# Block 2's local attention split into scores, division and values, and an earlier read-back of its outputs

## The chip, the cores and the metric

One Trainium2 chip, one core. The metric is the device time in microseconds of one launch of the whole program: the median of the runs shown, and the time of the profiled execution beside it.

## The reference

Two transformer blocks over 1024 tokens of width 1024, in float32. Block 1 is a linear-recurrence branch, a differential attention and a mixture of experts; the change doesn't touch it. Block 2 projects the normed input to queries, keys and values of two attentions, joins their outputs, projects them back and ends in an MLP of width 4096. The attention that the change is about has 8 query heads on 2 key heads, blocks of 128 queries, and sees the block itself and the one before:

```python
def swa_sinks_attention(q, k, v, sinks):
    ...
    scores = jnp.einsum('bnqkgd,bnskd->bnkgqs', qb, kb).astype(jnp.float32) * scale
    ...
    scores = scores + alibi[None, None]
    scores = jnp.where(valid[None, :, None, None], scores, -jnp.inf)
    ...
    m = jnp.maximum(jnp.max(scores, axis=-1, keepdims=True), sink)
    p = jnp.exp(scores - m)
    denom = jnp.sum(p, axis=-1, keepdims=True) + jnp.exp(sink - m)
    p = (p / denom).astype(v.dtype)
    out = jnp.einsum('bnkgqs,bnskd->bnqkgd', p, vb)
...
def second_block(x, ...):
        ...
        out_a = swa_sinks_attention(qa, ka, va, sink_logits)
        ...
        out_b = forgetting_attention(qb, kb, vb, log_f)
        mixed = jnp.concatenate([out_a.reshape(b, s, A_Q_W), out_b.reshape(b, s, B_W)], axis=-1)
        x = x + jnp.einsum('bse,ed->bsd', mixed, w_out)
        hn = rmsnorm(x, mlp_norm_g)
        hid = jnp.square(jax.nn.relu(jnp.einsum('bsd,df->bsf', hn, w_up)))
        x = x + jnp.einsum('bsf,fd->bsd', hid, w_down)
```

## The kernel before, in words

**Order of the work.** No scheduler of the language decides the order. The kernel is written as Python generators ("tasks", class `Tasks`, L424). When the program is built, a planner (class `Model`, L40, and class `Engine`, L207) keeps an estimated clock for each engine, runs the task of the smallest priority number whose next operands it holds to be ready, and appends the instructions to the engines' streams. What a task yields is either a time (operands ready) or a condition. On the chip every engine then works through its own fixed stream and waits where an operand is late. The dense products of block 2 belong to the task of priority 9 and so fill what the attention tasks leave; the splitting of weights into two halves for the products (`Stream._split`, L589: one ACT copy, one DVE subtraction of 128x1024) is held back while ACT or DVE have much work queued by the planner's clock.

**Precision.** Each operand of a product is split into a high and a low part (a Copy on ACT, a subtraction on DVE: `split`, `split_T`), and each product is three matmuls, hh, hl, lh.

**Block 2** (`block2`, L2007) goes over the two halves of 512 tokens. In each half it makes the keys, values and queries of both attentions. `fox(half)` and `fox_values(half)` (L2296, L2415) are the full-length forgetting attention, `swa(half)` (L2165) the local one. All write their outputs to the DRAM tensor `d_mix`; `mixin(half)` (L2489) reads them back as eight 128x512 slices, splits each, and sets a flag, on which `out2(half)` (L2522) makes the output projection. Then the MLP of the first half (`mlp`, L2583) runs while `swa(1)` and then `fox(1)` are worked in between its products; `fox(1)` starts only after `swa(1)`.

**Inside `swa`** (L2165 to L2294), for a block n of 128 queries:

- `prep(n)` (L2208): 4 transposes of the queries, split into `t`.
- `scores(n)` (L2219): two steps z of 12 matmuls for 2 heads of both key heads; for each head a reduction on DVE (scale, bias, minimum; CUSTOM_DVE in the profile, 128x256), a small DVE multiplication, and an Exp on ACT that also sums the row.
- `values(n, kh)` (L2248), for each of two key heads: a sink term, a sum, a reciprocal and one DVE multiplication of 128x1024 that divides the probabilities; then for each of 2 key blocks 4 transposes and a split (ACT 128x512, DVE 128x512); then 4 matmuls, an ACT copy and a DVE addition of 64x512, and the store to `d_mix`.

One generator does all this in one sequence, since `nsr = 2` (L2172): the probabilities have two buffers, so `values(n-1, 0)`, `values(n-1, 1)` are finished before `scores(n)` begins:

```python
        for n in range(n0, n0 + 5):
            if n > n0 and nsr == 2:
                for kh in range(2):
                    yield from values(n - 1, kh)
            if n < n0 + 4:
                yield from scores(n)
```

`mixin(0)` is added as a task at L2087, after the values of half 1 have been projected, and waits for `swa0` or the first pair of heads of `fox(0)` (L2492).

Of the kernel before, what the change touches and what calls it, by code (L numbers as in the profile page):

```python
# [285 lines left out]
class Buf:  # L286
# [25 lines left out]
    def free(self):  # L312
        self.arena.release(self)
# [344 lines left out]
class Kern:  # L658
# [1348 lines left out]
    def block2(self):  # L2007
        F, R, io, v, act = self.F, self.R, self.io, self.v, self.act
# [58 lines left out]
        ready = lambda tt: lambda: self.has(f"x2T{tt}")  # L2067
        for half in range(2):
# [16 lines left out]
            if half == 0:  # L2085
                self.tasks.add(self.fox(0), 1)
            else:  # L2087
                self.tasks.add(self.mixin(0), 4)
                nq = 2
                yield from self.dense_N(U["qa", 1], lhs, banks, evac_norm(self.QA, True), tts=tts[:nq])  # L2090
                yield from self.out2(0)
                tts = tts[nq:]
# [3 lines left out]
            if half == 0:  # L2096
                self.tasks.add(self.swa(0), 2)
        for b in (ring, raws, sm, bf, self.r2):
            b.free()
# [65 lines left out]
    def swa(self, half):  # L2165
# [4 lines left out]
        n0 = 4 * half  # L2170
        k0 = max(n0 - 1, 0)
        nsr = 2  # L2172
        nk = n0 + 4 - k0
        yield lambda: (self.has(f"qa{half}") and self.ws.settled() and self.F.fits(256 * nk, 512, 512, 32, 32, 32, 32, 512, *[1024] * nsr) and
                       self.R.fits(256 * nk, 256 * nk, 1024, 1024, 1024, 1024))
        S, tb, ob = Banks(self.psum, 2, 2), Banks(self.psum, 4, 2), self.bank(6)
        kT, V = R.alloc(2 * 128 * nk), R.alloc(256 * nk)
# [3 lines left out]
        qr, qT, pt = Ring(F, 2, 512), Ring(R, 2, 1024), Ring(R, 2, 1024)  # L2181
        st, orr = Ring(F, 4, 32), Ring(F, 1, 512)
        self.sp.dma_start(kv.f(nk, 256), self.KVA[k0 * 128:(n0 + 4) * 128].rearrange("(a p) c -> p a c", p=128))
        qs, Q, P = {}, {}, {}

# [19 lines left out]
        kv.free()  # L2205
        sr = Ring(F, nsr, 1024)

# [11 lines left out]
        def scores(n):  # L2219
# [4 lines left out]
            ks = slice(e - w, e)  # L2224
            bs, ss = [sr.next(), sr.next()], [st.next(), st.next()]
            for z in range(2):
# [18 lines left out]
            for kh in range(2):  # L2245
                P[n, kh] = (bs[kh], ss[kh], w)

        def values(n, kh):  # L2248
            b, s, w = P.pop((n, kh))
            f = s.f()  # L2250
            x = b.f(4, 256)[:, :, :w]
            yield W(f)
            v.tensor_tensor(f[:, 8:12], f[:, 8:12], snk.f()[:, 4 * kh:4 * kh + 4], OP.add)
            act.activation(f[:, 8:12], f[:, 8:12], AF.Exp)
            v.tensor_tensor(f[:, 8:12], f[:, 8:12], f[:, 4:8], OP.add)
            v.reciprocal(f[:, 12:16], f[:, 8:12])
            v.tensor_tensor(x, x, f[:, 12:16, None].to_broadcast([128, 4, w]), OP.mult)
            yield W(b.f())
            nb = w // 128
            ts = []  # L2260
            for c in range(nb):
                p, t = tb.next(), pt.next()
                yield free(p)
                for j in range(4):
                    self.pe.transpose(p[:, j * 128:j * 128 + 128], b.f(4, 256)[:, j, c * 128:c * 128 + 128], self.ident)
                self.split_T(p, t.r(2, 512)[:, 0], t.r(2, 512)[:, 1], t.f(2, 512)[:, 0])
                ts.append(t)
            yield max(W(ts[-1].f()), free(ob))
            for c in range(nb):
                vv = V.r(nk, 2, 128)[:, n + 1 - nb + c - k0, kh]  # L2270
                self.mm(ob, vv, ts[c].r(2, 512)[:, 0], c == 0, False)
                self.mm(ob, vv, ts[c].r(2, 512)[:, 1], False, c == nb - 1)
            yield W(ob)
            t = orr.next()
            act.activation(t.f()[0:64], ob[64:128], AF.Copy)
            v.tensor_tensor(t.f()[0:64], t.f()[0:64], ob[0:64], OP.add)
            self.sp.dma_start(self.MIX[256 * kh:256 * kh + 256, n * 128:n * 128 + 128].rearrange("(h d) t -> d h t", d=64),
                              t.f(4, 128)[0:64])

        yield from prep(n0)  # L2280
        for n in range(n0, n0 + 5):
            if n > n0 and nsr == 2:
                for kh in range(2):
                    yield from values(n - 1, kh)
            if n < n0 + 4:
                yield from scores(n)
                if n + 1 < n0 + 4:
                    yield from prep(n + 1)
            if n > n0 and nsr == 4:
                for kh in range(2):  # L2290
                    yield from values(n - 1, kh)
        for b in (kT, V, qr, qT, sr, pt, st, orr) + ((bias, snk, g) if half else ()):
            b.free()
# [195 lines left out]
    def mixin(self, half):  # L2489

        F, R = self.F, self.R
        yield lambda: self.has(f"swa{half}") or self.has(f"fox{half}0")  # L2492
        yield lambda: F.fits(512, 512, 512) and R.fits(*([1024] * 6 if half else [8192]))
# [335 lines left out]
```

## Time and profile before

| | |
|---|---|
| median of 3 runs | 2784.4 us (2781.36 to 2788.27) |
| the profiled execution | 2780.47 us, its span 2778.7 us |
| PE busy | 2642.0 us, 95% of the span |
| DVE busy | 1785.0 us, 64% |
| ACT busy | 1507.8 us, 54% |
| mean granted TensorE clock | 0.979 |

PE is TensorE's matmuls, PEld its weight loads, DVE is VectorE, ACT is ScalarE, POOL is GpSimd, SP is SyncE, which issues the DMAs. Since almost all work on chip passes two helper lines (L234 for TensorE, L270 for the other engines), work is told apart by tiles and shapes and by where it stands in the streams. Block 2 begins near 1527 us. The bounds of its stages, used below, were found by counting TensorE's instructions from the end of the program: the streams of the built kernel and of the trace agree there instruction for instruction. A busy time is that of a profile: an instruction may start a little before the one ahead of it has ended.

### The profile page before, as it was taken

What the parts mean: (1) busy time and instruction counts of PE and PEld (TensorE: products, weight loads), DVE (VectorE), ACT (ScalarE), POOL (GpSimd) and SP (SyncE); (2) the same over time, 40 slices, a digit from 0 to 9 for tenths busy, and PEclk for the clock granted to TensorE, in tenths of its full rate; (3) what the DMA queues carried; (4) which work ended last, traced back from release to release, by engine and by line L of the source; (5) the groups of instructions that cost most, each with busy time, mean ns of one, the idle gap of its engine ahead of it and who ended that gap; (6) DMA issues with size and microseconds to landing.
All of it is one profiled execution on the core that took longest, in us unless ns stands there. A gap on an engine that the chain in (4) does not pass through costs nothing. (4 is left out here: it accounts for less than half of the span.)

```text
span 2778.7 us, 37066 instructions
## 1 busy us (share of the span) xinstructions
PE 2642.0 (95%) x13090; PEld 2146.4 (77%) x13090; DVE 1785.0 (64%) x3100; ACT 1507.8 (54%) x2455; POOL 422.5 (15%) x486
## 2 busy tenths in 40 slices
PE   8899999999999799999997898889999999999999
PEld 6677777778888678888886776667887778888887
DVE  4574443652575699999986647755666666546683
ACT  4144444543443588888886646645545555345542
POOL 0540002430121113111111322200000000000000
PEclk9999999999999899999999999899999999999999
DMA  5333223435556899999997444444234443443330
GB/s 180 119 98 92 92 74 106 133 107 174 192 178 226 281 344 376 373 361 358 365 358 261 165 143 138 128 146 150 88 113 145 132 144 120 148 140 122 122 120 32
DMA packets 272030, 496.22 MB, mean 179 GB/s; under 512 B 30337, under 2 KB 127265, under 8 KB 271841
## 3 DMA queue, kind: packets, MB, share of 16 engines
q1 hardware_dynamic: 261184, 471.78, 49.7%
q0 software_dynamic: 9216, 16.81, 2.4%
q10 hardware_dynamic: 1440, 5.24, 0.5%
q8 instruction: 103, 1.69, 0.3%
q14 instruction: 87, 0.70, 0.1%
HBM read 440.05 MB, written 70.45 MB: 184 GB/s over the span
## 5 line engine op out<-in xcount | busy, mean ns | idle before, releaser
L234 PE MATMUL psum<-rounded,swing 128*128 128x512 f32 (+1 forms) x3552 | 868.4, 396 | 23.4 <-ACT swing L270 10.3
L234 PE MATMUL psum<-rounded 128*128 128x512 f32 (+6 forms) x3672 | 791.8, 386 | 24.3 <-DVE rounded L270 11.3
L234 PE MATMUL psum<-swing,rounded 128*128 128x512 f32 (+1 forms) x3328 | 785.0, 389 | 0.4 <-DVE swing L270 0.4
L234 PEld LDWEIGHTS psum<-rounded,swing 128*128 128x128 f32 x3552 | 651.5, 192 | 166.3 <-issue 18.4
L234 PEld LDWEIGHTS psum<-rounded 128*128 128x128 f32 (+1 forms) x3672 | 609.4, 189 | 174.0 <-issue 19.8
L270 DVE TENSOR_TENSOR rounded<-exact,rounded 128x1024 fp32r<-128x1024 f32 (+1 forms) x483 | 572.2, 1206 | 234.4 <-ACT rounded L270 226.8
L234 PEld LDWEIGHTS psum<-swing,rounded 128*128 128x128 f32 x3328 | 603.8, 189 | 129.2 <-issue 6.5
L270 ACT ACTIVATE rounded<-exact 128x1024 fp32r<-128x1024 f32 (+1 forms) x483 | 500.6, 1045 | 296.6 <-PE psum L234 221.1
L234 PE MATMUL psum<-exact 128*128 128x128 f32 (+6 forms) x2198 | 312.9, 284 | 78.0 <-DVE exact L270 23.4
L234 PEld LDWEIGHTS psum<-exact 128*128 128x128 f32 (+2 forms) x2198 | 262.5, 163 | 141.4 <-DVE exact L270 36.1
L270 POOL TENSOR_TENSOR exact<-exact 128x1 f32<-128x1 f32 (+6 forms) x272 | 261.2, 964 | 721.4 <-DMA exact<-d_cb 416.6
L270 ACT ACTIVATE exact<-psum 128x512 f32<-128x512 f32 (+4 forms) x290 | 160.1, 553 | 366.0 <-PE psum L234 297.3
L270 ACT ACTIVATE exact<-exact 128x512 f32<-128x512 f32 (+11 forms) x398 | 247.1, 632 | 175.7 <-DVE exact L270 147.4
L270 DVE TENSOR_TENSOR rounded<-swing,rounded 128x1024 fp32r<-128x1024 f32 x217 | 256.4, 1218 | 37.9 <-ACT rounded L270 37.0
L270 ACT ACTIVATE rounded<-swing 128x1024 fp32r<-128x1024 f32 x217 | 223.8, 1065 | 36.3 <-PE psum L234 26.4
L270 DVE TENSOR_TENSOR exact<-psum,exact 128x512 f32<-128x512 f32 x156 | 107.3, 688 | 143.3 <-PE psum L234 111.8
L270 DVE TENSOR_TENSOR exact<-exact 128x512 f32<-128x512 f32 (+9 forms) x250 | 154.6, 628 | 42.4 <-POOL exact L270 24.1
L270 DVE CUSTOM_DVE_ANT_0 exact<-psum,exact 128x512 f32<-128x512 f32 (+5 forms) x224 | 127.8, 593 | 80.4 <-PE psum L234 51.6
L270 POOL TENSOR_SCALAR exact<-exact 128x1 f32<-128x1 f32 (+4 forms) x134 | 42.6, 318 | 785.4 <-DVE exact L270 553.1
L270 DVE TENSOR_TENSOR swing<-psum,swing 128x512 fp32r<-128x512 f32 (+2 forms) x151 | 88.9, 615 | 95.1 <-ACT swing L270 94.7
L270 ACT ACTIVATE rounded<-psum 128x512 fp32r<-128x512 f32 (+2 forms) x190 | 88.1, 496 | 105.8 <-PE psum L234 105.2
L270 DVE TENSOR_TENSOR rounded<-psum,rounded 128x512 fp32r<-128x512 f32 (+2 forms) x190 | 101.7, 558 | 56.4 <-ACT rounded L270 56.3
(49 smaller groups left out, 1074.1 us busy)
## 6 DMA issues: line engine op xcount, KB each, us to landing
exact<-in_w_dram SPq DMA_DIRECT2D x188, 512.0 KB
swing<-in_w_dram SPq DMA_DIRECT2D x186, 512.0 KB
exact<-in_w_in_dram SPq DMA_DIRECT2D x72, 512.0 KB
exact<-in_w_down_dram SPq DMA_DIRECT2D x66, 512.0 KB
exact<-in_w_up_dram SPq DMA_DIRECT2D x62, 512.0 KB
exact<-in_w_out_dram SPq DMA_DIRECT2D x32, 512.0 KB
exact<-in_x_dram SPq DMA_DIRECT2D x16, 512.0 KB
d_g<-exact SPq DMA_DIRECT2D x32, 256.0 KB
```

Of the source, the lines that this page charges most:

```text
L234: r = fn(*args, **kw)
L270: r = fn(*args, **kw)
```

## The change

`swa` becomes three tasks. `swa` keeps the queries and the scores; `swa_scale` divides; `swa_values` transposes, multiplies and stores, with the products of one key block issued after the transposes of the next, and the last copy and addition one step later still. The probabilities get four buffers instead of two, handed on by `take` and `give`. `mixin(0)` is added right after `swa(0)` and waits for `swa0` alone.

```diff
@@ block2
-                self.tasks.add(self.mixin(0), 4)
                 nq = 2
...
             if half == 0:
                 self.tasks.add(self.swa(0), 2)
+                self.tasks.add(self.mixin(0), 4)
@@ swa
-        nsr = 2
+        nsr = 4
...
-        sr = Ring(F, nsr, 1024)
+        sr = Slots(F, nsr, 1024)
+        sx = {"V": V, "k0": k0, "nk": nk, "sr": sr, "st": st, "pt": pt, "orr": orr, "ready": {}, "scaled": {}}
+        steps = [(n, kh) for n in range(n0, n0 + 4) for kh in range(2)]
+        self.tasks.add(self.swa_scale(steps, sx), 1)
+        self.tasks.add(self.swa_values(half, steps, sx), 1)
...
-            bs, ss = [sr.next(), sr.next()], [st.next(), st.next()]
+            bs, ss = [], []
+            for kh in range(2):
+                bs.append((yield from sr.take()))
+                ss.append((yield from st.take()))
...
+    def swa_scale(self, steps, sx):
+
+        v, act, snk, W = self.v, self.act, self.snk, self.model.written
+        for n, kh in steps:
+            yield lambda: (n, kh) in sx["ready"]
+            b, s, w = sx["ready"].pop((n, kh))
             f = s.f()
             x = b.f(4, 256)[:, :, :w]
             yield W(f)
...
             v.tensor_tensor(x, x, f[:, 12:16, None].to_broadcast([128, 4, w]), OP.mult)
...
+            sx["st"].give(s)
+            sx["scaled"][n, kh] = b
...
+        def multiply():
+            if state[0] is None:
+                return
+            (n, kh), c, nb, t = state[0]
+            state[0] = None
+            yield max(W(t.f()), free(ob) if c == 0 else 0.0)
+            vv = V.r(nk, 2, 128)[:, n + 1 - nb + c - k0, kh]
+            self.mm(ob, vv, t.r(2, 512)[:, 0], c == 0, False)
+            self.mm(ob, vv, t.r(2, 512)[:, 1], False, c == nb - 1)
...
+        for n, kh in steps:
+            nb = 2 if n else 1
+            for c in range(nb):
+                if (n, kh) not in sx["scaled"]:
+                    yield from finish()
+                    yield from multiply()
+                    yield lambda: (n, kh) in sx["scaled"]
+                b = sx["scaled"][n, kh]
+                p, t = tb.next(), pt.next()
+                yield max(free(p), W(b.f()))
+                for j in range(4):
+                    self.pe.transpose(p[:, j * 128:j * 128 + 128], b.f(4, 256)[:, j, c * 128:c * 128 + 128], self.ident)
+                self.split_T(p, t.r(2, 512)[:, 0], t.r(2, 512)[:, 1], t.f(2, 512)[:, 0])
+                if c == nb - 1:
+                    sx["sr"].give(b)
+                yield from finish()
+                yield from multiply()
+                state[0] = (n, kh), c, nb, t
@@ mixin
-        yield lambda: self.has(f"swa{half}") or self.has(f"fox{half}0")
+        yield lambda: self.has(f"swa{half}") or half and self.has(f"fox{half}0")
```

No instruction is added or taken away; all that changes is where they stand. Three places of the streams, first as they were, then as they are. In them `exact` is the arena of plain float32, `rounded` and the numbered `swing` buffers hold split operands. On TensorE a product 128x512 out of `rounded` with a `swing` is a dense product with weights, `rounded 128x256 x12` is a step of local scores, `exact 128x128 x4` are transposes, and two or four products of 128x512 out of `swing_10935` named first (in `swa(1)`), or of `swing_10934` alone (in `swa(0)`), are local values.

The first place is on TensorE in `swa(1)`, from a scores step on, before:

```order
L234 MATMUL psum<-rounded 128x256 x12
L234 MATMUL psum<-rounded,swing_10935 128x512 x18
L234 MATMUL psum<-rounded 128x256 x12
L234 MATMUL psum<-exact 128x128 x4
L234 MATMUL psum<-rounded,swing_10935 128x512 x27
L234 MATMUL psum<-swing_10934,rounded 128x512 x12
L234 MATMUL psum<-exact 128x128 x8
L234 MATMUL psum<-swing_10934,rounded 128x512 x15
L234 MATMUL psum<-swing_10935,rounded 128x512 x4
```

And with the change:

```order
L234 MATMUL psum<-rounded 128x256 x12
L234 MATMUL psum<-swing_10934,rounded 128x512 x3
L234 MATMUL psum<-swing_10935,rounded 128x512 x2
L234 MATMUL psum<-exact 128x128 x4
L234 MATMUL psum<-swing_10935,rounded 128x512 x2
L234 MATMUL psum<-exact 128x128 x4
L234 MATMUL psum<-rounded 128x256 x12
L234 MATMUL psum<-exact 128x128 x4
L234 MATMUL psum<-swing_10935,rounded 128x512 x2
L234 MATMUL psum<-exact 128x128 x4
```

Between two steps of the attention stood 12 to 27 dense products; now there are 3 or none.

The second place is on TensorE in `swa(0)`, where it meets the products of half 1 (of 264 and 512 columns) and `fox(0)` (`rounded 128x384`), before:

```order
L234 MATMUL psum<-rounded,swing_10935 128x264 x6
L234 MATMUL psum<-rounded 128x256 x6
L234 MATMUL psum<-exact 128x128 x2
L234 MATMUL psum<-rounded,swing_10935 128x512 x15
L234 MATMUL psum<-exact 128x128 x4
L234 MATMUL psum<-rounded,swing_10935 128x512 x3
L234 MATMUL psum<-exact 128x128 x3
L234 MATMUL psum<-rounded 128x384 x6
L234 MATMUL psum<-swing_10934 128x512 x2
```

And with the change:

```order
L234 MATMUL psum<-swing_10934 128x256 x12
L234 MATMUL psum<-rounded 128x256 x6
L234 MATMUL psum<-exact 128x128 x6
L234 MATMUL psum<-swing_10934 128x256 x12
L234 MATMUL psum<-exact 128x128 x4
L234 MATMUL psum<-rounded,swing_10935 128x264 x3
L234 MATMUL psum<-exact 128x128 x7
L234 MATMUL psum<-rounded 128x384 x6
L234 MATMUL psum<-rounded 128x256
```

The next scores of `swa(0)` (`swing_10934 128x256 x12`) now stand where dense products stood, which come later.

The third place is on SP, which issues the DMAs, around the last read-backs of `d_mix` and the first loads of `out2(0)` (`d_x`), before:

```order
L221 DMA d_mix<-exact 64x4x128
L221 DMA exact<-d_mix 128x512
L221 DMA exact<-in_w_out_dram 128x2x512
L221 DMA exact<-d_mix 128x512
L221 DMA exact<-in_w_out_dram 128x2x512
L221 DMA d_qa<-exact 128x512
L221 DMA exact<-in_w_in_dram 128x2x512
L221 DMA exact<-d_mix 128x512 x2
L221 DMA d_qa<-exact 128x512
L221 DMA exact<-d_mix 128x512 x3
L221 DMA exact<-d_x_4491 128x512 x2
```

And with the change:

```order
L221 DMA d_mix<-exact 64x256
L221 DMA exact<-d_mix 128x512
L221 DMA d_vb<-exact 128x512
L221 DMA exact<-in_w_out_dram 128x2x512 x2
L221 DMA d_vb<-exact 128x512
L221 DMA exact<-in_w_out_dram 128x2x512 x3
L221 DMA exact<-d_x_4491 128x512 x3
```

Seven of the eight read-backs have moved ahead into `fox(0)`, and only that of the last pair of heads is left here.

## Rows read from the trace of the kernel before

**Rows 1.** The page, parts 1 (busy us, share, instructions) and 2 (busy tenths in slices).

```profile
PE 2642.0 (95%) x13090; PEld 2146.4 (77%) x13090; DVE 1785.0 (64%) x3100; ACT 1507.8 (54%) x2455; POOL 422.5 (15%) x486
...
DVE  4574443652575699999986647755666666546683
```

**Rows 2.** Windows, by stages of block 2: length, busy us, granted clock, DMA share, GB/s.

```profile
core 0: us, PE busy (x) PEld busy (x) DVE busy (x) ACT busy (x) POOL busy (x), PEclk, DMA share, GB/s
...
1677.70:1724.30 46.60, 37.96 (x236) 30.23 (x235) 32.55 (x110) 29.04 (x86) 10.85 (x16) 0.96 0.47 128
1724.30:1770.80 46.50, 36.53 (x183) 28.11 (x182) 36.69 (x94) 27.69 (x64) 10.86 (x14) 0.85 0.39 105
1770.80:1816.30 45.50, 41.87 (x231) 33.05 (x230) 35.37 (x111) 29.43 (x80) 9.96 (x12) 0.92 0.42 122
...
1845.20:1866.00 20.80, 12.57 (x35) 8.02 (x36) 11.47 (x15) 8.18 (x12) 2.20 (x2) 0.67 0.60 201
...
1916.30:1940.00 23.70, 20.50 (x86) 16.51 (x85) 11.52 (x17) 12.67 (x21) 1.84 (x2) 0.87 0.66 217
1940.00:2072.30 132.30, 132.30 (x677) 108.12 (x676) 88.88 (x212) 74.48 (x163) 0.00 (x0) 1.00 0.29 85
2072.30:2149.10 76.80, 74.39 (x401) 59.25 (x401) 49.66 (x99) 37.67 (x67) 4.59 (x10) 1.00 0.52 155
...
2278.40:2343.50 65.10, 64.54 (x351) 51.70 (x350) 43.16 (x89) 33.50 (x60) 2.76 (x6) 1.00 0.37 118
2343.50:2372.40 28.90, 28.87 (x128) 23.59 (x127) 15.01 (x20) 11.01 (x15) 0.00 (x0) 1.00 0.43 139
```

**Rows 3.** Windows, stages put together.

```profile
1677.70:1816.30 138.60, 116.37 (x648) 91.39 (x647) 104.62 (x313) 86.16 (x229) 31.67 (x42) 0.91 0.43 118
...
1677.70:1885.50 207.80, 177.30 (x903) 139.17 (x902) 137.82 (x361) 113.49 (x272) 35.71 (x46) 0.91 0.45 134
1916.30:2072.30 156.00, 152.80 (x761) 124.63 (x760) 100.40 (x229) 87.16 (x183) 1.84 (x2) 0.98 0.34 105
1838.30:1885.50 47.20, 38.93 (x152) 29.49 (x151) 20.86 (x25) 15.39 (x20) 4.04 (x4) 0.86 0.59 195
```

**Rows 4.** Timeline 1834 to 1866, output projection of half 0: start, us, engine, what.

```profile
1849.79 2.07 PE L234 MATMUL psum<-rounded,swing 128*128 128x512 f32 x4 [1.40 <-DVE swing L270]
...
1853.51 0.32 SPq L221 DMA_DIRECT2D d_qa<-exact  x1
1853.93 5.20 SPq L221 DMA_DIRECT2D exact<-d_mix  x3
1856.78 1.27 ACT L270 ACTIVATE swing<-exact 128x512 fp32r<-128x512 f32 x2 [7.51 <-DMA exact<-d_mix]
...
1857.46 8.75 PE L234 MATMUL psum<-rounded,swing 128*128 128x512 f32 x26 [5.60 <-ACT swing L270]
```

**Rows 5.** Waits of PE, 1677.7 to 1838.3.

```profile
PE psum L234 <- DVE rounded L270: 15.5, 10, 3.3
PE psum L234 <- DVE exact L270: 3.9, 3, 1.6
```

**Rows 6.** Waits of SP, 1677 to 1816.

```profile
SPq L221 <- DVE exact L270: 77.0, 42, 6.3
```

**Rows 7.** Groups of DVE by form, 1916.3 to 2072.3.

```profile
L270 DVE TENSOR_TENSOR rounded<-exact,rounded 128x1024 fp32r<-128x1024 f32 x25 | 30.4, 1223 | 10.6 <-ACT rounded L270 10.6
...
L270 DVE TENSOR_TENSOR exact<-psum,exact 128x512 f32<-128x512 f32 x17 | 11.7, 687 | 3.9 <-PE psum L234 3.8
```

**Rows 8.** Groups of PE by form, 1916.3 to 2072.3.

```profile
L234 PE MATMUL psum<-swing,rounded 128*128 128x512 f32 x368 | 89.9, 400 | 0.0
...
L234 PE MATMUL psum<-exact 128*128 128x128 f32 x85 | 12.2, 283 | 3.2 <-DMA exact<-d_kva 1.8 <-DVE rounded L270 1.4
```

**Rows 9.** Windows of 20 us inside the first stage.

```profile
1740.00:1760.00 20.00, 14.29 (x53) 10.90 (x52) 15.63 (x38) 11.72 (x24) 5.21 (x8) 0.66 0.49 146
1760.00:1780.00 20.00, 18.78 (x123) 14.89 (x121) 16.73 (x57) 13.79 (x42) 2.52 (x4) 1.00 0.21 50
```

More of the change, by code (lines that the diff above doesn't have):

```diff
@@ L2171, in swa @@
         k0 = max(n0 - 1, 0)
-        nsr = 2
+        nsr = 4
         nk = n0 + 4 - k0
-        yield lambda: (self.has(f"qa{half}") and self.ws.settled() and self.F.fits(256 * nk, 512, 512, 32, 32, 32, 32, 512, *[1024] * nsr) and
+        yield lambda: (self.has(f"qa{half}") and self.ws.settled() and self.F.fits(256 * nk, 512, 512, 32, 32, 32, 32, 512, *[1024] * (nsr - nk // 4)) and
                        self.R.fits(256 * nk, 256 * nk, 1024, 1024, 1024, 1024))
-        S, tb, ob = Banks(self.psum, 2, 2), Banks(self.psum, 4, 2), self.bank(6)
+        S, tb = Banks(self.psum, 2, 2), Banks(self.psum, 4, 2)
         kT, V = R.alloc(2 * 128 * nk), R.alloc(256 * nk)
@@ L2181, in swa @@
         qr, qT, pt = Ring(F, 2, 512), Ring(R, 2, 1024), Ring(R, 2, 1024)
-        st, orr = Ring(F, 4, 32), Ring(F, 1, 512)
+        st, orr = Slots(F, 4, 32), Ring(F, 1, 512)
         self.sp.dma_start(kv.f(nk, 256), self.KVA[k0 * 128:(n0 + 4) * 128].rearrange("(a p) c -> p a c", p=128))
-        qs, Q, P = {}, {}, {}
+        qs, Q = {}, {}
         def load(n):
@@ L2245, in scores @@
             for kh in range(2):
-                P[n, kh] = (bs[kh], ss[kh], w)
-        def values(n, kh):
-            b, s, w = P.pop((n, kh))
+                sx["ready"][n, kh] = bs[kh], ss[kh], w
+        yield from prep(n0)
+        for n in range(n0, n0 + 4):
+            yield from scores(n)
+            if n + 1 < n0 + 4:
+                yield from prep(n + 1)
+        for b in (kT, qr, qT) + ((bias, g) if half else ()):
+            b.free()
+    def swa_scale(self, steps, sx):
[3 more added lines that the diff above has]
+            b, s, w = sx["ready"].pop((n, kh))
             f = s.f()
@@ L2257, in values, with swa_values, finish @@
             v.tensor_tensor(x, x, f[:, 12:16, None].to_broadcast([128, 4, w]), OP.mult)
[L2258 to L2272, printed above, removed]
+            sx["st"].give(s)
+            sx["scaled"][n, kh] = b
+    def swa_values(self, half, steps, sx):
+        v, act = self.v, self.act
+        W, free = self.model.written, self.model.released
+        V, k0, nk, pt = sx["V"], sx["k0"], sx["nk"], sx["pt"]
+        tb, ob = Banks(self.psum, 4, 2), self.bank(6)
+        state = [None, None]
+        def multiply():
[8 more added lines that the diff above has]
+            if c == nb - 1:
+                state[1] = n, kh
+        def finish():
+            if state[1] is None:
+                return
+            n, kh = state[1]
+            state[1] = None
             yield W(ob)
-            t = orr.next()
+            t = sx["orr"].next()
             act.activation(t.f()[0:64], ob[64:128], AF.Copy)
@@ L2278, in values @@
                               t.f(4, 128)[0:64])
[L2280 to L2292, printed above, removed]
+        for n, kh in steps:
[11 more added lines that the diff above has]
+                self.split_T(p, t.r(2, 512)[:, 0], t.r(2, 512)[:, 1], t.f(2, 512)[:, 0])
+                if c == nb - 1:
+                    sx["sr"].give(b)
+                yield from finish()
+                yield from multiply()
+                state[0] = (n, kh), c, nb, t
+        yield from finish()
+        yield from multiply()
+        yield from finish()
+        for b in (V, sx["sr"], pt, sx["st"], sx["orr"]) + ((self.snk,) if half else ()):
             b.free()
```

## The prediction

> **What bounds the kernel now.** I read the page first. TensorE is busy for 95% of the span and DVE for 64% [rows 1], and the change neither adds nor removes an instruction; so only time that TensorE waits, or works at its lower clock, can be won or lost. Next I read the windows by stage of block 2, where the change moves work [rows 2]. Two kinds of stage stand there. From 1677.7 to 1816.3, where `fox(0)` and `swa(0)` run together, TensorE is busy for 116.37 of 138.60 us at a granted clock of 0.91, and DVE for 104.62 [rows 3]: neither engine is full, each waits for the other. From 1940.0 to 2072.3, where `swa(1)` runs between products of the MLP, TensorE is busy for all of 132.30 us at full clock, with DVE at 88.88 [rows 2]: there TensorE alone sets the time, and no rearrangement can win anything. Between them lies a plain hole: from 1845.2 to 1866.0 TensorE is busy for 12.57 of 20.80 us at clock 0.67 [rows 2]. The timeline tells its cause [rows 4]: the store of `d_qa` holds SP until 1853.51, the last three read-backs of `d_mix` are issued after it, ACT waits 7.51 us for one to land, and the output projection waits 5.60 us for ACT. Last I read who lets TensorE wait in the first stage: DVE's subtractions, 15.5 us in ten waits, then DVE's other results, 3.9 us [rows 5].
>
> **Prices.** A dense product of 512 columns in an unbroken run costs 28.87/128 = 0.226 us, as from 2343.5 on [rows 2]; in `swa(1)` it was 89.9/368 = 0.244 with other work between [rows 8], but it is moved to where it runs unbroken, so 0.226 holds. A transpose costs 12.2/85 = 0.144 us [rows 8], which I also take for the other small matmuls. A weight split costs DVE 1.223 us, an evacuation of 512 columns 0.687 us [rows 7]. Counted in the order of the two programs, `swa(1)` stands among 759 matmuls before (546 of them dense), with 24 weight splits and 32 evacuations on DVE; with the change among 420 (207 dense), with 10 splits and 12 evacuations. So its own DVE work is 100.40 [rows 3] less 30.4 for the splits [rows 7] less 32 x 0.687 = 22.0, which is 48.0 us for 138 instructions, 0.348 us each.
>
> **swa(1), a loss.** 339 dense products leave the stage and come after `fox(1)`. What remains for TensorE is 152.80 - 339 x 0.226 = 76.2 us, for DVE 100.40 - 14 x 1.223 - 20 x 0.687 = 69.5 us. The first 23.7 us, with 20.50 and 11.52 us of it [rows 2], keep their order. Behind them remain 55.7 us of TensorE and 58.0 us of DVE. Before, these 55.7 us cost just themselves, since the products hid every wait; the order now shows at most three products between two steps. So the stretch lasts 58.0/u, where u is the share of the time that DVE can be kept busy. The trace has no stretch like it. The bounds are the shares of the first stage, 36.69/46.5 = 0.79 and 35.37/45.5 = 0.78 [rows 2], and a nearly full DVE, 0.95, since the page has slices, in block 1's experts, with DVE at nine tenths or more [rows 1]. The nearest row is the best 20 us of that stage, 16.73/20 = 0.84 [rows 9]; since three sequences give DVE something else to do when one waits, I take 0.86. That is 67.4 us, **11.7 us more** than before; 5 to 19 us between the bounds. The moved products win nothing later: the stages after run at 0.97 to 1.00 of TensorE [rows 2], and from `fox(1)` on the same work follows, with the same small waits.
>
> **swa(0), a gain.** From 1677.7 to 1885.5, 207.8 us [rows 3], the same work is cut into three parts.
> (a) To the end of `swa(0)`: 385 matmuls, 102 dense; on DVE 125 instructions of the local attention, 43.5 us, 4 splits, 4.9 us, and 63 others. Their price comes from the first stage: 104.62 - 12 x 1.223 - 108 x 0.348 = 52.4 us over 145 instructions, 0.361 us each, so 22.7. DVE's 71.1 us at u = 0.86 make 82.7 us, more than TensorE's 102 x 0.226 + 283 x 0.144 = 63.8.
> (b) To the end of `fox(0)`'s scores: 181 dense products and 119 small ones, 40.9 + 17.1 = 58.0 us, with fewer DVE instructions (98) than (a); between 76.80/74.39 = 1.03 times that, as beside `fox(1)`, and 45.5/41.87 = 1.09, as beside `fox(0)` [rows 2], that is 59.7 to 63.2; I take 62, nearer to `fox(0)`.
> (c) To the first finished tile of `out2(0)`: 216 dense products, 48.8 us; 49 to 51, I take 50. Seven of the eight read-backs are done inside `fox(0)`, and the last is issued more than 60 products (14 us) ahead of its use, against the 7.51 us that the slowest took [rows 4]. This is where the hole goes: before, 1838.3 to 1885.5 took 47.2 us for 150 dense products [rows 3] worth 33.9, an excess of 13.3.
> Together 194.7 us, **13.1 us less**. Most is the hole; the 22 us that TensorE waited in the first stage are about kept, since DVE is now the late one in (a).
>
> **What costs nothing.** The two further buffers fit into the arena when `swa` has freed its keys and values. On SP the DMAs are as many as before; the read-backs now stand ahead of weight loads and wait for stores that wait for DVE. SP waited 77.0 us for DVE in this stage already [rows 6] with the DMA engines at 0.43 [rows 3], and the weight loads run ahead of their use; without that cover a late weight would hold products for some us, which the range holds.
>
> [...] In the first stage TensorE waited ten times for a subtraction while DVE was busy for 104.62 of 138.60 us [rows 3, 5]: the awaited one stood behind others. [...] By the rows alone u may rise or not; I take 0.86.
>
> **The sum.** -13.1 + 11.7 = -1.4 us. The profiled execution took 2780.47 us, 3.9 less than the median of 2784.4; on the median the forecast is **2783 us**. With 112 us for (b) and (c) the net is 129.1/u - 151.5, so u decides all. A measurement here can tell about 0.3%, 8.4 us, from no change; the net is inside that from u = 0.90 down to 0.81.
>
> **Rivals.**
> 1. *DVE stays fed, faster.* For it: 20 us at 0.84 with one local sequence alone [rows 9], and no transfer in the way. Against: DVE's long instructions wait for ACT's copies. At u = 0.95 with 59.7 and 49: 74.8 + 59.7 + 49 - 207.8 = -24.3, and 61.1 - 55.7 = +5.4; net -18.9, **2766 us**. Chance 0.32.
> 2. *The cover is gone, slower.* In `swa(1)` every late subtraction now holds TensorE's stream, and the products behind it. For it: 0.78 and 0.79 in a stage with as much attention [rows 2], and ten waits for DVE [rows 5]; against: those came with one local sequence. At u = 0.78 with 63.2 and 51: 91.2 + 114.2 - 207.8 = -2.4, and 74.4 - 55.7 = +18.7; net +16.3, **2801 us**. It decides below u = 0.81. Chance 0.17.
> 3. *The lower clock.* [...] Chance 0.06.
> 4. *It doesn't remove the hole.* A late store of `fox(0)`'s last pair of heads, or SP held by one, keeps `out2(0)` waiting: (c) grows by up to 13.3, net +11.9, **2796 us**. Chance 0.07.
>
> **How the numbers follow.** My forecast, u between 0.81 and 0.90, has 0.38. Faster by over 0.3% is rival 1, 0.32; slower are rivals 2 to 4, 0.30. The range goes from just under rival 1's time, 2765, to rival 2's, 2801; it leaves out u over 0.95 and two slower cases at once, some 2 in 10.
>
> **What would show it.** Right: a stretch of some 67 us after 1940 with DVE at 0.86 and TensorE waiting for DVE at several places, no ACT wait for `d_mix` before `out2(0)`, and after `fox(1)` an unbroken run of some 440 products, 100 us. Wrong: a TensorE that is still full in `swa(1)`, a first stage whose waits shrink by more than the hole, or a clock under 0.8 in (a).

## The result, and the profile after

The change made the kernel slower: 2811.58 us median of four executions (2806.23 to 2814.62) against 2785.66 of before beside them (2781.36 to 2788.27), a ratio of 1.0093 with a 95% interval of 1.0071 to 1.0114. That is 25.9 us more; the forecast was 2783 us, and its range ended at 2801.

The windows of the changed kernel, cut at the ends of the prediction's parts and stages (found by counting matmuls from the end of the program); columns: start and end, length, busy us and count of each engine, granted clock, DMA share, GB/s:

```profile
core 0: us, PE busy (x) PEld busy (x) DVE busy (x) ACT busy (x) POOL busy (x), PEclk, DMA share, GB/s
1685.50:1774.50 89.00, 70.72 (x387) 53.75 (x386) 68.08 (x234) 55.93 (x169) 14.49 (x20) 0.81 0.33 89
1774.50:1845.60 71.10, 60.27 (x302) 48.17 (x301) 47.54 (x106) 40.34 (x84) 18.37 (x22) 0.95 0.52 149
1845.60:1894.60 49.00, 49.00 (x218) 40.58 (x217) 20.29 (x22) 17.53 (x20) 4.58 (x4) 1.00 0.59 191
...
1925.40:1949.10 23.70, 20.62 (x92) 16.49 (x92) 11.49 (x17) 13.11 (x22) 1.84 (x2) 0.93 0.67 216
1949.10:2027.50 78.40, 63.16 (x334) 49.48 (x333) 58.31 (x179) 45.73 (x124) 0.00 (x0) 0.89 0.17 50
...
2306.20:2406.20 100.00, 100.00 (x442) 82.80 (x442) 43.89 (x53) 40.20 (x54) 0.00 (x0) 1.00 0.35 114
```

The first three rows are the parts (a), (b) and (c) of the prediction: 209.1 us together, against 207.8 before [rows 3] and 194.7 forecast. The hole is gone, since (c) is full. Then comes `swa(1)`: its first 23.7 us are as before [rows 2], and its rest takes 78.4 us, where 67.4 were forecast. Before, the stage took 156.0 us [rows 3]; 339 of its dense products, 76.6 us, now come later, so 79.4 would have cost nothing, and it takes 102.1: **22.7 us lost**. The moved products then run full, 100 us, as forecast. The profiled execution took 2814.62 us, 34.2 more than that of before; 7.8 of it lie ahead of the first moved instruction, in the same order of work, and 1.3 + 22.7 + 2 (in `fox(1)`, beyond 24 of the moved products that now stand there) behind it.

Who lets TensorE wait in those 78.4 us, and who VectorE (views of waits, 1949.1 to 2027.5: us in total, times, longest):

```profile
PE psum L234 <- DVE exact L270: 9.0, 6, 3.3
PE psum L234 <- DVE swing L270: 6.2, 3, 2.9
```
```profile
DVE swing L270 <- ACT swing L270: 7.6, 7, 1.9
DVE rounded L270 <- ACT rounded L270: 5.9, 5, 1.8
DVE exact L270 <- ACT exact L270: 5.1, 10, 1.1
DVE exact L270 <- PE psum L234: 2.9, 3, 1.5
```

TensorE waits 15.2 us for VectorE, and VectorE 18.6 us for ScalarE: a ring of short steps. Followed back from the end of the stretch, from each step to what released it, the chain of work lies on VectorE for 28.3 us, on TensorE for 24.9 and on ScalarE for 20.6; in the other 4.6 an engine waited for nothing that the profile shows. The stage is not quite bare: of its 162 matmuls of 128x512 in this stretch 32 are values, and the other 130 are dense products, in runs of up to 18. One piece of the ring in the timeline (start, us, engine, what, in brackets the idle time before and its releaser):

```profile
2010.18 2.36 DVE L270 TENSOR_TENSOR exact<-exact 128x1024 f32<-128x1024 f32 x2
2012.46 0.67 DVE L270 TENSOR_TENSOR exact<-exact,psum 64x512 f32<-64x512 f32 x1
...
2013.19 1.22 PE L234 MATMUL psum<-swing,rounded 128*128 128x512 f32 x2 [3.35 <-DVE exact L270]
```

The addition that empties the values' PSUM bank stands behind two division products, and the next product waits 3.35 us for it.

### The profile page after: what moved, and what is told of

Its sections match the earlier page's. It is cut to its first block, busy times and chain, and to the rows that moved or that the text cites. A ratio compares the mean times of both kernels' runs of the same rounds, so it can differ in the third digit from the quotient of the medians.

```text
span 2812.8 us, 37080 instructions
## 1 busy us (share of the span) xinstructions
PE 2659.0 (95%) x13090; PEld 2159.9 (77%) x13090; DVE 1782.2 (63%) x3100; ACT 1510.5 (54%) x2455; POOL 430.7 (15%) x486
## 5 line engine op out<-in xcount | busy, mean ns | idle before, releaser
L234 PE MATMUL psum<-rounded,swing 128*128 128x512 f32 (+1 forms) x3552 | 859.6, 394 | 14.6 <-DVE exact L270 10.6
L234 PE MATMUL psum<-swing,rounded 128*128 128x512 f32 (+2 forms) x3328 | 794.9, 391 | 6.9 <-DVE exact L270 5.4
L270 DVE TENSOR_TENSOR rounded<-exact,rounded 128x1024 fp32r<-128x1024 f32 (+2 forms) x483 | 571.4, 1206 | 244.1 <-ACT rounded L270 236.7
L270 ACT ACTIVATE rounded<-exact 128x1024 fp32r<-128x1024 f32 (+2 forms) x483 | 500.6, 1045 | 308.3 <-PE psum L234 243.6
L234 PE MATMUL psum<-exact 128*128 128x128 f32 (+6 forms) x2198 | 324.6, 289 | 95.1 <-DVE exact L270 30.3
L234 PEld LDWEIGHTS psum<-exact 128*128 128x128 f32 (+2 forms) x2198 | 269.3, 166 | 163.9 <-DVE exact L270 43.3
L270 ACT ACTIVATE swing<-psum 128x512 fp32r<-128x512 f32 (+2 forms) x151 | 77.2, 537 | 116.7 <-PE psum L234 116.1
```

Source lines behind the costliest of these rows:

```text
L234: r = fn(*args, **kw)
L270: r = fn(*args, **kw)
```

## The experiments

Ratios are to the kernel before, measured beside each. "First part" is from `fox(0)`'s first write to `out2(0)`'s first tile (901 matmuls), in the profiled execution; in `swa(1)` the last column adds 0.226 us for each dense product that the kernel moved behind it (156.0 before).

| kernel | median us | ratio, 95% interval | first part | swa(1) | with moved products |
|---|---|---|---|---|---|
| changed | 2811.58 | 1.0093, 1.0071 to 1.0114 | 209.1 | 102.1 | 178.7 |
| swa(0) alone | 2784.17 | 1.0009, 0.9996 to 1.0022 | 206.9 | 154.8 | 154.8 |
| swa(1) alone | 2806.87 | 1.0080, 1.0059 to 1.0100 | 203.6 | 103.3 | 179.9 |
| swa(1) paced | 2790.60 | 1.0032, 1.0017 to 1.0047 | 207.2 | 129.6 | 159.4 |
| stores on GpSimd | 2805.74 | 1.0076, 1.0058 to 1.0094 | 206.1 | 102.4 | 179.0 |
| narrow division | 2802.92 | 1.0071, 1.0057 to 1.0084 | 205.6 | 93.4 | 170.0 |
| two banks | 2810.41 | 1.0101, 1.0085 to 1.0116 | 205.6 | 104.2 | 180.8 |
| filler | 2811.47 | 1.0104, 1.0089 to 1.0120 | 206.2 | 102.7 | 179.3 |
| bare, one sequence | 2859.98 | 1.0281, 1.0258 to 1.0303 | 200.8 | 109.9 | 233.3 |
| bare, three | 2840.55 | 1.0204, 1.0175 to 1.0232 | 207.1 | 83.6 | 207.0 |
| read-backs on GpSimd | 2785.18 | 1.0003, 0.9992 to 1.0014 | 199.7 | 155.3 | 155.3 |
| swa(0), late read-back | 2789.38 | 1.0024, 1.0012 to 1.0035 | 211.9 | 155.9 | 155.9 |
| swa(0) paced | 2800.79 | 1.0062, 1.0041 to 1.0083 | 220.6 | 153.4 | 153.4 |
| swa(0), division on GpSimd | 2780.76 | 0.9993, 0.9981 to 1.0006 | 205.1 | 155.3 | 155.3 |
| before, division on GpSimd | 2787.68 | 1.0009, 0.9993 to 1.0025 | 207.8 | 156.6 | 156.6 |

### Where the loss is: swa(0) alone, swa(1) alone

```diff
-        self.tasks.add(self.swa(1), 2)
+        self.tasks.add(self.swa_one(1), 2)
```

> Change: the changed kernel, but swa(1) goes back to the single sequence of before; swa(0) keeps its three sequences and mixin(0) its earlier place. The two traces, lined up by counting matmuls, put the first part (fox(0)'s first write to out2(0)'s first tile) at 209.1 us against 207.8 before, and swa(1), after taking off 339 dense matmuls at 0.226 us, at +22.7 us. Theory 1 (the loss is made in swa(1), where the dense products no longer stand between two waits): this kernel is within 0.2% of before, about 2787 us beside 2785.7, and in its trace the stretch of swa(1) is as long as before. The prediction's steps (a shorter first part is there, and something else in the program costs it back): about 2773 us, 13 us under before. A loss that sits in the first part: 2795 us or more.

The other half, in the kernel before (`swa_three` is the changed `swa`):

```diff
-        self.tasks.add(self.swa(1), 2)
+        self.tasks.add(self.swa_three(1), 2)
```

> Change: the kernel before, with the three sequences in swa(1) alone; swa(0) and mixin(0) stay as they were. Theory 1: the whole loss is here, 22 to 26 us over before, so about 2809 us; after the first 23.7 us of swa(1) TensorE waits some 15 us for VectorE and the stretch takes 76 to 80 us. If the loss of the changed kernel needs both halves (memory, queues or the state that swa(0) leaves behind), this one is within 5 us of before.

The first kernel has the old single sequence in `swa(1)`. With the change in `swa(0)` alone the time is that of before; with it in `swa(1)` alone the loss is all there, 24 us by the medians and 22 by the ratio. So Theory 1's place is right, and the gain that the prediction's steps gave to the first part does not exist.

### Cover given back: swa(1) paced

```diff
             for z in range(2):
+                if half:
+                    yield self.model.now() + 9000.0
                 sb = [S.next() for _ in range(2)]
```

> Change: the changed kernel, but in swa(1) each scores step (two head pairs, 8 times) is put 9.0 us of the planner's own clock behind the one before, so that the planner lays dense matmuls between them again: 207 more of them stand before swa(1)'s last instruction than in the changed kernel, where 339 fewer stand than in before. The three sequences themselves are as in the changed kernel. Theory 1 (the dense products were the cover, and a chain of VectorE, ScalarE and TensorE steps lies bare without them): most of the 22.7 us comes back, 2787 to 2795 us. Rival 2 (SyncE stands at a store for VectorE and holds up what it has to load): the stores are still behind the same VectorE instructions, at most a third comes back, 2803 us or more. Rival 3 (VectorE's load as such): the load over the stretch is diluted by the added matmuls but its sum is the same; with VectorE at 0.74 of the stretch before, it would come back too, so this run does not tell 1 from 3.

Windows of this kernel, the first 23.7 us of `swa(1)` and its rest, then TensorE's waits in the rest:

```profile
1921.80:1945.50 23.70, 20.59 (x90) 16.71 (x89) 11.49 (x17) 13.10 (x22) 1.84 (x2) 0.93 0.66 216
1945.50:2051.40 105.90, 103.47 (x541) 81.76 (x540) 77.16 (x199) 60.31 (x143) 0.00 (x0) 1.00 0.26 82
```
```profile
PE psum L234 <- DVE exact L270: 1.9, 5, 0.5
PE psum L234 <- DVE swing L270: 0.4, 2, 0.2
```

With 207 products back between the steps, TensorE waits 2.3 us in place of 15.2 and runs at a granted clock of 1.00; of `swa(1)`'s 22.7 us 19.3 are back. What is left is 3.4 us here and some 4.5 in `fox(1)` (277.7 us against 271.2, of which 9 more matmuls are 2.0). The latter proves nothing: with read-backs on GpSimd, where TensorE, VectorE and ScalarE keep the order of before in `fox(1)`, it took 278.5.

### Not SyncE's queue: stores on GpSimd

```diff
-            self.sp.dma_start(self.MIX[...
+            (self.gp if half else self.sp).dma_start(self.MIX[...
```

> Change: the changed kernel, but swa(1)'s stores to MIX are issued by GpSimd's queue in place of SyncE's, so that a store that waits for VectorE holds up no load on SyncE. In the changed kernel SyncE waits 53.1 us there for tile exact, in 8 waits, the longest 19.9 us. Rival 2 (SyncE's wait is the loss): swa(1) is back at its time of before, 2787 us. Theory 1: TensorE waited there for VectorE alone and for no DMA, so the time stays at 2809 to 2813 us, while SyncE's waits for exact all but go.

`swa(1)` took 102.4 us, as in the changed kernel. SyncE's wait did not go, against what was expected: with the stores away it stood as long at a weight load whose buffer VectorE had still to release. Its waits, 1940.9 to 2019.6:

```profile
SPq L221 <- DVE exact L270: 51.8, 2, 42.7
```

So the edit did not take away what it was made to take away. What speaks against SyncE is that TensorE waited for no transfer meanwhile, in this kernel as in the changed one: all its waits here, 8.8 and 5.7 us, are for VectorE. With that the rival of these two expectations that blames SyncE's queue falls.

### VectorE's share: narrow division

```diff
+            few = None
+            if sx["half"]:
+                few = (x[:, :, :16], x[:, :, :16], f[:, 12:16, None].to_broadcast([128, 4, 16]), OP.mult)
-            v.tensor_tensor(x, x, f[:, 12:16, None].to_broadcast([128, 4, w]), OP.mult)
+            v.tensor_tensor(x, x, f[:, 12:16, None].to_broadcast([128, 4, w]), OP.mult, emit=few)
```

> Change: the changed kernel with every engine's order kept, but in swa(1) the division multiplies 16 of the up to 256 columns of each head, so most of that division is left out. VectorE loses about 8.6 us of its 58.3 us in the stretch of 78.4 us (8 products of 1218 ns, which become some 0.14 us each). If VectorE's load as such sets the stretch, at an unchanged share of 0.74 it shrinks by 8.6/0.74 = 11.6 us: about 2797 us if the changed kernel is at 2809. If TensorE's waits are a chain of steps through VectorE and ScalarE, in which these products stand ahead of what TensorE waits for only now and then (6 waits for tile exact, 9.0 us), it shrinks by 3 to 7 us: 2802 to 2806 us. If the lower clock alone is the loss: no change.

The rest of `swa(1)` in this kernel:

```profile
1941.00:2010.70 69.70, 60.18 (x340) 47.24 (x339) 50.30 (x178) 46.82 (x126) 0.00 (x0) 0.95 0.19 57
```

VectorE works 8.0 us less and the stretch is 8.7 us shorter; the medians differ by some 6 to 9. So the work of these eight products counts about one for one, between the two figures expected: they stood on the path. VectorE as a whole does not stand there all the time: the chain followed back lies on it for 16.4 of the 69.7 us (28.3 of 78.4 in the changed kernel). It is busy for 0.72 of the stretch, no more than before (0.74), so it is not its load alone: with less to do it still waits.

### Not one late bank, not the clock: two banks, filler

```diff
-        tb, ob = Banks(self.psum, 4, 2), self.bank(6)
+        tb, obs = Banks(self.psum, 4, 2), Banks(self.psum, 6, 2 if half else 1)
...
+            if c == 0:
+                state[2] = obs.next()
+            ob = state[2]
             yield max(W(t.f()), free(ob) if c == 0 else 0.0)
```

> Change: the changed kernel, but in swa(1) the products with the values go to two PSUM banks in turn, where one bank had to be emptied by VectorE before the next product could start. The same 420 matmuls stand in swa(1); the planner draws some of them in another order. In the changed kernel a wait of 3.35 us at 2013.19 is of this kind: VectorE's addition that empties the bank stood behind two division products of 2.36 us. If single waits of this kind are the loss (first in, first out behind long instructions): 4 to 8 us back, swa(1) at 94 to 98 us. If VectorE and ScalarE are too late all over the stretch: the wait moves to the next thing that TensorE needs, within 3 us of the changed kernel.

`swa(1)` took 104.2 us; the waits went elsewhere (TensorE's, 1942.7 to 2023.2):

```profile
PE psum L234 <- DVE exact L270: 6.4, 3, 3.8
PE psum L234 <- DVE swing L270: 4.8, 2, 2.7
PE psum L234 <- ACT swing L270: 3.6, 1, 3.6
```

The filler, in the changed kernel:

```diff
             yield max(W(t.f()), free(ob) if c == 0 else 0.0)
+            for j in range(4 * half):
+                self.pe.eng.transpose(self.bank(7)[:, j * 128:j * 128 + 128], self.ident, self.ident)
```

> Change: the changed kernel with every engine's order kept, but ahead of each of the 16 products of values in swa(1) TensorE transposes the identity four times into an unused bank: 64 small matmuls more, some 10 us of TensorE time, that nobody reads and that need nothing. They lie where TensorE idles now. If the granted clock of 0.89 is a good part of the loss (63.16 us of busy time against 55.7 at full clock, so 7.5 us): the clock goes to 0.97 or more and swa(1) is 4 to 7 us shorter. If it is the waits that set the time: the clock rises, but swa(1) stays within 3 us of 102 us, since TensorE then only waits less. If the filler delays the steps themselves: up to 10 us longer.

The rest of `swa(1)`:

```profile
1944.70:2023.70 79.00, 66.84 (x401) 54.17 (x400) 58.36 (x179) 46.69 (x125) 0.00 (x0) 0.96 0.18 55
```

The clock rose from 0.89 to 0.96, and the stretch stayed at 79.0 us (78.4). Raising the clock in this way wins nothing. But the filler has a time of its own:

```profile
L2295 PE MATMUL psum<-exact 128*128 128x128 f32 x64 | 10.5, 291 | 0.0
```

Followed back from the end, the chain runs through 5.2 us of it. So this run does not show that the lower clock costs nothing: what a higher clock gave back, the filler may have taken. In the trace of the changed kernel the granted clock is 1.00 from 2002 to 2010 and 0.50 from 2012 to 2018; a product of 128x512 took 396 to 468 ns in the first of these stretches and 677 to 706 in the second (means by group, of products that overlap). The chain lies on TensorE for some 9.7 us at 0.50, so my estimate, from 0.50 against 1.00, is that the clock costs at most half of that, some 5 of the 22.7 us.

### All cover taken away: one sequence and three

Both kernels, in the task of the dense products:

```diff
+        yield lambda: self.has("swa1")
         self.model.phase(5)
         yield from self.mlp()
```

> Change: the kernel before (one sequence), with the MLP's products held until swa(1) has ended, so that swa(1) has no cover at all: 213 matmuls in place of 759. The 546 dense products that leave it are worth 546 x 0.226 = 123.4 us elsewhere, so swa(1) would have to take 32.6 us to cost nothing. Theory 1 (cover is what matters, and the three sequences shorten a bare chain): one bare sequence is the longest of all, some 100 us, so about 2850 us. If the three sequences themselves make swa(1) slow (VectorE's queue mixed from three heads): one bare sequence is no longer than three, under 80 us, 2831 us or less.

> Change: the changed kernel (three sequences), with the MLP's products held in the same way: the same 213 matmuls in swa(1). Theory 1: shorter than one bare sequence by 15 us or more, but VectorE's own 48 us at the 0.74 measured in the changed kernel, with some 15 us of start ahead of it, is 80 us, far over 32.6: about 2831 us. If the three sequences hold each other up in VectorE's queue: as long as one bare sequence, or longer.

All of `swa(1)`, first in one sequence, then in three:

```profile
1916.10:2026.00 109.90, 53.44 (x215) 36.86 (x215) 54.21 (x174) 38.43 (x116) 1.84 (x2) 0.53 0.16 47
```
```profile
1919.20:2002.80 83.60, 46.69 (x215) 34.57 (x215) 52.62 (x175) 40.48 (x118) 1.84 (x2) 0.63 0.17 51
```

Three sequences do what they were made for: 83.6 us where one takes 109.9, and TensorE waits 17.8 us for tile `exact` in place of 41.7 (it is also busy for 6.75 us less, at a granted clock of 0.63 in place of 0.53):

```profile
PE psum L234 <- DVE exact L270: 41.7, 12, 6.2
```
```profile
PE psum L234 <- DVE exact L270: 17.8, 13, 2.9
```

But a bare stage may take only 32.6 us to cost nothing, and covered by 546 products, one sequence cost nothing. What the change did to `swa(1)` is this: it took away 339 products of cover that hid everything, and put an order in their place that hides a part. One sequence with the changed kernel's 207 dense products was not run, so how much the three save there is open.

### The first part: the read-back, the pace, the division

Read-backs on GpSimd, in the kernel before:

```diff
-            self.sp.dma_start(b.f(), self.MIX[...
+            (self.sp if half else self.gp).dma_start(b.f(), self.MIX[...
```

> Change: the kernel before, with the eight read-backs of d_mix in mixin(0) issued by GpSimd's queue in place of SyncE's; TensorE's, VectorE's and ScalarE's orders stay as they were. In before the last three read-backs stand behind a store of d_qa that holds SyncE until 1853.51, ScalarE waits 7.51 us for one, and the output projection's stretch of 47.2 us is 13.3 us over its 150 dense products. If SyncE's queue is the cause of this hole: 6 to 13 us under before, 2770 to 2777 us. On GpSimd's queue the last four stand behind norm instructions that end at about 1852.7, so less than that may come, 1 to 6 us. If the read-backs wait for their data or buffers and not for the queue: within 1 us of before.

No gain in the medians. From the end of `fox(0)`'s scores to `out2(0)`'s first tile it took 67.9 us, 69.2 before; its shorter first part comes from the 131.8 us ahead of that, whose order is the same as before's (138.6 [rows 3]). With `swa(0)` ending where it did before, another queue does not help.

In the kernel with three sequences in `swa(0)` alone, the read-back put back where it was:

```diff
             else:
+                self.tasks.add(self.mixin(0), 4)
                 nq = 2
...
                 self.tasks.add(self.swa(0), 2)
-                self.tasks.add(self.mixin(0), 4)
```

> Change: the kernel with three sequences in swa(0) alone (swa(1) in one, as before), and mixin(0) started where it was before the change, so the two parts of the change in the first stage are taken apart: the earlier end of swa(0) stays, the earlier read-back goes. mixin(0)'s last transposes then stand at matmul 8244 in place of 8181, as in before. If the early read-back is what took the hole away and that hole cost 13 us: 5 to 13 us over the kernel with both parts (1.0009 of before), so 2790 to 2797 us. If the time that TensorE waits in the first stage only moves from one place to another: within 3 us of that kernel, 2782 to 2788 us.

(a), (b) and (c) with the early read-back, then with the late one:

```profile
1682.30:1771.40 89.10, 71.42 (x386) 54.81 (x386) 68.85 (x235) 55.66 (x168) 14.54 (x20) 0.81 0.34 91
1771.40:1840.20 68.80, 60.10 (x301) 47.83 (x301) 46.72 (x105) 40.08 (x83) 18.40 (x22) 0.95 0.52 151
1840.20:1889.20 49.00, 49.00 (x218) 40.62 (x217) 20.29 (x22) 17.53 (x20) 4.58 (x4) 1.00 0.56 188
```
```profile
1677.30:1764.50 87.20, 66.69 (x387) 50.64 (x386) 67.88 (x234) 55.70 (x169) 13.66 (x20) 0.88 0.34 91
1764.50:1828.50 64.00, 59.58 (x302) 48.07 (x301) 43.44 (x99) 37.03 (x76) 17.33 (x22) 0.95 0.48 137
1828.50:1889.20 60.70, 53.01 (x217) 41.49 (x217) 25.04 (x29) 21.60 (x27) 3.68 (x4) 0.92 0.54 184
```

The hole is worth 60.7 - 49.0 = 11.7 us, near the 13.3 of the prediction, and the early read-back does take it away; but its copies and subtractions now fall into (b), which is 4.8 us longer (66.7 to 71.1 us in the eight kernels that keep the changed order of the first part, 64.0 here). Net 5 us in these two executions, 4 by the ratios (1.0024 to 1.0009), whose intervals overlap: half a gain, near the lower end of what was expected if the hole counts.

In the same kernel, `swa(0)`'s scores steps put 7.0 us apart:

```diff
             for z in range(2):
+                yield self.model.now() + 7000.0
                 sb = [S.next() for _ in range(2)]
```

> Change: the kernel with three sequences in swa(0) alone, and in swa(0) each scores step is put 7.0 us of the planner's clock behind the one before, so that more products of the neighbours stand between them: swa(0) ends at matmul 7995 (7848 without, 8214 before), mixin(0)'s last transposes at 8154. If the dense products are cover that a stage can use only once, the waits go from swa(0) to what follows and the first part (fox(0)'s first write to out2(0)'s first tile) stays at 204 to 209 us: 2782 to 2787 us. If the order was the fault: some of the 30 us that TensorE is not busy there come back, the first part takes 195 to 201 us, 2773 to 2779 us.

220.6 us, worse than either expectation. Up to the end of `swa(0)`, VectorE was busy for 91.52 of 131.7 us, a share of 0.69. What pacing gave back in `swa(1)`, it took here. That there were few independent products to put between is the reading nearest to hand; no run shows it.

The division on GpSimd, once with three sequences in `swa(0)` (the edit shown), once in the kernel before (the same in `values`, for `swa(0)` alone):

```diff
-            v.tensor_tensor(x, x, f[:, 12:16, None].to_broadcast([128, 4, w]), OP.mult)
+            self.gp.tensor_tensor(x, x, f[:, 12:16, None].to_broadcast([128, 4, w]), OP.mult)
```

> Change: the kernel with three sequences in swa(0) alone, and the division's product of swa(0) (8 times, 2 of 512 and 6 of 1024 columns, 8.5 us of VectorE) is made by GpSimd. In swa(1), leaving out 8.0 us of the same VectorE work made that stretch 8.7 us shorter. If VectorE's queue sets the pace of swa(0) in the same way: 6 to 9 us under the kernel without, 2775 to 2779 us. If GpSimd takes much longer for one product than VectorE's 1.22 us, the values come later and TensorE waits for GpSimd instead: no gain, or up to 8 us slower.

> Change: the kernel before, one sequence, with the division's product of swa(0) on GpSimd. With one sequence the product stands between scores and values of the same step; what GpSimd takes longer than VectorE is waited for unless the neighbours fill it. If VectorE's load of 104.6 us in the stage of 138.6 us is what keeps TensorE waiting: 4 to 8 us under before. If the length of the chain of steps is: 0 to 8 us over.

GpSimd's groups in `swa(0)` of the first:

```profile
L270 POOL TENSOR_TENSOR exact<-exact 128x1024 f32<-128x1024 f32 x6 | 12.1, 2028 | 10.2 <-PE psum L234 8.4 <-DVE exact L270 1.7
```

One product takes GpSimd 2028 ns, VectorE some 1217, and TensorE waited 2.8 us for GpSimd. The first kernel has the lowest median ratio of all, 0.9993, which is not told apart from before, nor from the 1.0009 without the edit; the 6 to 9 us expected did not come. The second is at 1.0009. No version was found that beats the kernel before.

## Why the prediction was wrong

**What failed first is u, the share of the time for which VectorE is kept busy without cover.** I took 0.86, above the best 20 us of the first stage, 0.84 [rows 9], and held 0.78 for the lower bound [rows 2]. Measured: 58.31/78.4 = 0.74 in `swa(1)` and 68.08/89.0 = 0.76 in (a). My own rows held that figure: the first stage as a whole has 104.62/138.60 = 0.755 [rows 3], and the first of its thirds, which I left out of the bounds, 32.55/46.6 = 0.70 [rows 2]. So the mechanism was rival 2, "the cover is gone", with a chance of 0.17, and even its price was too low. The parts together came out 25.4 us over the forecast: u accounts for 11.0 in `swa(1)` and 6.3 in (a), (b) for 9.1, and (c) for 1.0 the other way. That the formula 129.1/u - 151.5 gives +23.0 us at 0.74, near the 25.9 measured, is in part luck, since its 112 us for (b) and (c) were 120.1.

**swa(1), +11.7 forecast, +22.7 measured.** VectorE's work was right (58.0 against 58.31), and so were the moved products (100 us). The choice within the bounds was wrong: a best stretch of 20 us is no measure for a stage of 78, and "three sequences give VectorE something else to do" was an argument without a row. The bare pair shows that the argument itself is true, 26.3 us of it, and far too small. The form was too simple as well: dividing VectorE's work by a share makes it the path, and the chain lies on it for only 28.3 of the 78.4 us, TensorE and ScalarE having the most of the rest. "At most three products between two steps" was read off one extract of the order (the barest, 1977 to 1991 in the trace); elsewhere in the stretch stand runs of up to 18.

**swa(0), -13.1 forecast, +1.3 measured** (about +3 by the mean of eight kernels that keep the changed order of the first part, 206.7, against 204.1 in three with the old). (c) was right, 49.0 against 50. (a) took 89.0 in place of 82.7, with 3.0 us less of VectorE's work than I counted: u again (on the clock's part in it see below). (b) took 71.1 in place of 62: I priced it at 1.03 to 1.09 of TensorE's work, and did not count that the early read-back's copies and subtractions go there; the run with the late read-back, 64.0, shows that this is most of it.

**What costs nothing.** The SyncE step held: in the changed kernel TensorE waited for no transfer from 1685.5 to 1894.6, nor from 1949.1 to 2027.5.

**The order in VectorE's queue.** TensorE's wait of 3.35 us was for an addition that stood behind two division products of 2.36 us together. Rival 2 had u at 0.78; it went lower, and no run shows that the order in the queue is why: with a second bank the waits only moved (14.8 us in place of 15.2). Nor is it that more sequences hold each other up on balance: bare, three are 26.3 us shorter than one.

**The clock.** Rival 3, the lower clock, had a chance of 0.06, and under 0.8 in (a) was to show the forecast wrong; the clock was 0.81 there, and 0.89 in the rest of `swa(1)`. For (a) the runs give a price, since nine profiled executions have the same order there: in seven, at 0.79 to 0.83, TensorE was busy for 70.5 to 72.7 us and (a) took 89.0 to 90.6; with the late read-back and in the bare three, both at 0.88, it was busy for 66.7 and 66.9 us and (a) took 87.2 and 87.4. From the changed kernel to the late read-back that is 4.0 us of work less and 1.8 us of time; at that rate I estimate the clock's part in the 6.3 us that (a) was too long at some 3. In `swa(1)` the filler leaves it open, up to some 5 us by my estimate. In both stretches TensorE waits, 18.0 us in (a) and 15.2 in the rest of `swa(1)`, and the clock is below 1; in (c) and in the 100 us of moved products it doesn't wait, and the clock is 1.00.

## What to carry to other kernels

Before a stage is reordered to wait less, look whether it waits at all: the rest of `swa(1)` was full on TensorE, 132.30 of 132.30 us at a granted clock of 1.00 [rows 2], so its long chain cost nothing, and dense work that the new order moves out from beside it can turn the chain into time. Price a stage that loses its cover by the mean of the nearest stage and not by its best stretch, and let the range reach its worst: the mean of the first stage, 0.755, would have put the formula at +19.5 us, and its first third, 0.70, at +33. A hole that closes also sends its work somewhere: count what that place pays, here 4.8 us in (b) against 11.7 in (c).

## What the runs showed of the hardware

The same order of work need not take the same time: from `fox(0)`'s first write to the end of its scores, TensorE, VectorE and ScalarE have the same order in the kernel before and in that with read-backs on GpSimd, and took 138.6 us at a granted clock of 0.91 in one profiled execution and 131.8 at 0.96 in the other; two more kernels with that order took 135.4 at 0.94 and 134.6 at 0.96. So a difference of 7 us in one stage between two single profiles of this kernel proves nothing without the medians.

A higher granted clock need not shorten a stage by what it takes off TensorE's busy time. In the stage just named it came close: 116.37 us of work in 138.6 us at 0.91, 111.47 in 134.6 at 0.96. In part (a), in one order, 0.88 in place of 0.81 took 4.0 us off TensorE's work and 1.8 off the time. And 64 idle transposes raised the clock of `swa(1)` from 0.89 to 0.96, took 10.5 us of TensorE themselves, and the stage was as long as before. In the bare stages, where TensorE was busy for 53.44 of 109.9 and 46.69 of 83.6 us, it was granted a clock of 0.53 and 0.63.
